# An 8-head half of a projection by Strassen's seven products, in a hybrid S5/RG-LRU decoder layer on Trainium2

## The chip, the core and the metric

The kernel runs on one core of a Trainium2 chip. The metric is the device time of one execution in microseconds (us), as the median of several runs. A profiled execution gives a trace of every engine: TensorE (PE: matmuls; PEld: its weight loads), VectorE (DVE), ScalarE (ACT), GpSimd (POOL) and SyncE (SP), which here only issues DMAs. DMAs are also issued from POOL.

## The reference: what is computed

One decoder layer on 1024 tokens of width 1024, everything in float32. Two branches run side by side and are merged by gates:

```
h = rms_norm(x, g_pre)
s5_x, s5_g, lru_x, lru_g, gate_s, gate_l = split(h @ w_in)
glu_a, glu_b = split(gelu(s5_ssm(s5_x)) @ w_glu)             # 512 -> 2 x 512
z_s = (glu_a * sigmoid(glu_b) * silu(s5_g)) @ w_bs           # 512 -> 1024
y_l = rg_lru(causal_conv(lru_x))                             # 10 heads of 128
z_l = (y_l * silu(lru_g)) @ w_bl                             # 1280 -> 1024
merged = sigmoid(gate_s) * z_s + sigmoid(gate_l) * z_l
x = x + rms_norm(merged @ w_out, g_post)                     # 1024 -> 1024
x = x + (p @ w_ple) * sigmoid(x @ w_ple_gate)
```

The change is in `z_l`, the product with w_bl: 10 input blocks (the heads) by 8 output blocks (rows d = 0 to 7) of 128 x 128.

## The kernel before

**Layout.** Activations are kept transposed, channels on the 128 partitions and the 1024 tokens (NT) along the free dimension, in two halves of 512 (HT). A product of a weight block with half the tokens is one matmul of 128x128 by 128x512.

**Three matmuls for one.** Both sides are kept as a high part (rounded to the matmul's type fp32r) and a low part, the remainder. `three` (L307 to 311) issues high x high, high x low and low x high, so a row of w_bl for both halves is 10 heads x 2 halves x 3 = 60 matmuls, and all of w_bl 480. `split` makes the parts of an operand: the high part by ACT's copy, the low part by DVE's subtraction (L305).

**Weights** (class `Weights`, L124 to 246). All blocks lie in one array in the order of use. SP loads chunks of up to 8 blocks (512 KB, L157) into four raw buffers. Four blocks make a quad: ACT copies the high part (L216) and DVE subtracts the low part (L228) into a ring of six quads; for w_bs, w_out and w_ple_gate the low part is made by an ACT copy of the negative (L219) and an adding DMA issued from POOL (L220). `W.ahead()`, called before a quad's matmuls, makes the quad four further on, its low part with the call after, and fetches and sums beyond that.

**Strassen's products in w_out.** For w_out the kernel already uses the Winograd form of Strassen's scheme. A 2 x 2 arrangement is made of the operand (two halves of the rows k, two halves of the tokens: B11, B12, B21, B22) and of the weights of two output rows (A11 to A22). Seven products replace eight; the weight sums S1 to S4 are made on POOL (`sum`, L173 to 205, the addition at L188), the operand differences T1 to T4 on DVE, and the products go to PSUM banks of their own which DVE adds into SBUF.

**Order of the work.** PE, ACT, DVE and POOL run in the order in which the program lists the instructions; SP's order is chosen by a scheduler, and it runs in that order too, so that a DMA that waits holds those behind it. Small pieces of work for DVE and ACT are written as generators in a list `bg`; `tick()`, called between products, lets each go on by one step, and `drain()` finishes them. The stages on PE are: w_ple, w_in's S5 columns, the gates (with the S5 recurrence beside), the ten LRU heads, then

- w_bl rows 0 and 1 together and row 2 (`bl`, L1097 to 1109), while `gel_build` splits the S5 outputs (L1083 to 1092);
- w_glu, four pairs eb and ea (L1128 to 1141): ACT takes the sigmoid of eb, DVE multiplies ea into `ysf` (L1138), and both split it into `ys`;
- w_bl rows 3 to 7, each followed by DVE's product with its gate (L1108) and a store to DRAM (`ms_d`); `yl_last` fetches head 9 again, whose place was lent;
- w_bs, eight rows F (L1231 to 1236): DVE multiplies the row by its gate `sgs_d`, loaded one to three rows ahead, into `mg` (L1234), and a DMA from POOL adds the w_bl row from `ms_d` onto it (L1235); `merged` (L1207) splits the sums and makes the differences for w_out;
- w_out: the X products (oX), then oY, oZ, oW, oV for each pair of rows; then w_ple_gate.

The operands of w_bl, `yl`, are made by head: heads 0 to 5 inside the LRU stage (L1039 to 1042), 6 to 9 after its end (L1068 to 1074). Before that loop DVE still has the product of the last gate column (`sg`, L952).

**PSUM.** `px` holds two banks, `pw2` three tiles of two banks (`wide`). After the last row F, `pw2` is closed and a pool `pp` of six single banks is opened in its place (L1237 and 1238; `bank`, L313), so that the first bank can be written once everything in `pw2` has been read.

Of the kernel before, what the change touches and what calls it, by code (L numbers as in the profile page):

```python
# [36 lines left out]
def weight_plan():  # L37
# [39 lines left out]
    plain(col("w_in", 7, range(ND)))  # L77
    for d in range(ND):
        if d == 3:
            for j in range(NS):  # L80
                plain(col("w_glu", 4 + j, range(NS)) + col("w_glu", j, range(NS)))
        if d == 0:
            for ks in (range(0, 4), range(4, 8), range(8, 10)):
                plain(col("w_bl", 0, ks) + col("w_bl", 1, ks))
        elif d > 1:
            for ks in (range(0, 8), range(8, 10)):
                plain(col("w_bl", d, ks))
    for n in range(0, ND, 2):
# [158 lines left out]
def tile_hybrid_trunk(  # L247
# [14 lines left out]
    px = ctx.enter_context(tc.tile_pool(name="px", bufs=2, space=PSUM))  # L262
    wide_ctx = ExitStack()
    pw2 = wide_ctx.enter_context(tc.tile_pool(name="pw2", bufs=3, space=PSUM))
    W = Weights(ctx, tc, w)
# [3 lines left out]
    def page(i, name, dt=F32R):  # L269
        return page_pool[i].tile([P, 2 * NT], dt, tag=f"pg{i}", name=name)  # L270
# [5 lines left out]
    ms_d = dram.tile([ND, P, NT], F32, name="ms_d")  # L276
    yl_d = dram.tile([P, NT], F32, name="yl_d")
    u_d = dram.tile([NS, 8, 16, 8, P], F32, name="u_d")
# [33 lines left out]

    def bank(name):  # L313
        return pp.tile([P, HT], F32, tag="pp", name=name)

    def wide(name):
        return pw2.tile([P, NT], F32, tag="pw2", name=name)

    bg = []
# [658 lines left out]
    l1 = lctx.enter_context(tc.tile_pool(name="l1", bufs=1))  # L978
    yl_home = {m: i for m, i in enumerate((2, 3, 6, 7, 8, 9, 4, 5, 10, 11))}
    yl, yl_raw = {}, {}  # L980

    def yl_page(m):
        t = page(yl_home[m], f"yl{m}", F32).rearrange("p (s n) -> p s n", s=2)
        yl[m] = t.bitcast(F32R)
        return t

    def lru_head(m):
# [33 lines left out]
        def late():  # L1021
            S.activation(ta, r, AF.Tanh, scale=sp8[:, m:m + 1])
            V.tensor_tensor(i, i, c, ALU.mult)
            S.activation(r, r, AF.Exp, scale=nsp8[:, m:m + 1])
            S.activation(sq, r, AF.Square)
            yield
            V.scalar_tensor_tensor(ta, sq, 1.0, ta, ALU.add, ALU.mult)
            S.activation(ta, ta, AF.Sqrt)
            yield
            V.tensor_tensor(i, i, ta, ALU.mult)  # L1030
            V.tensor_tensor_scan(sq, r, i, 0.0, ALU.mult, ALU.add)
            yield
            t = l1.tile([P, NT], F32, tag=f"yr{m}", name=f"yr{m}") if m in (6, 7) else g
            V.tensor_tensor(t, sq, g, ALU.mult)
            yl_raw[m] = t
            if m == NL - 1:
                nc.sync.dma_start(yl_d, t)
            if m < 6:
                yl_page(m)  # L1039
                S.activation(yl[m][:, 0], t, AF.Copy)  # L1040
                yield
                V.tensor_tensor(yl[m][:, 1], t, yl[m][:, 0].bitcast(F32), ALU.subtract)

# [12 lines left out]
    def gel_load():  # L1056
        for i in range(2):
            gel.append(page(i, f"gel{i}", F32).rearrange("p (b n) -> p b n", b=2))
        for b in range(NS):
            v = gel[b // 2][:, b % 2].rearrange("p (j k) -> p j k", j=8)  # L1060
            for g in range(8):
                nc.sync.dma_start(v[16 * g:16 * g + 16], y_d[b][:, :, g].rearrange("j c k -> c j k"))
# [4 lines left out]
    gel_load()  # L1067
    for m in range(6, NL):  # L1068
        t = yl_page(m)
        if m % 2:  # L1070
            V.tensor_copy(yl[m][:, 0], yl_raw[m])
        else:
            S.activation(yl[m][:, 0], yl_raw[m], AF.Copy)
        V.tensor_tensor(yl[m][:, 1], yl_raw[m], t[:, 0], ALU.subtract)
    lctx.close()
# [17 lines left out]

    def ylr(k, h):
        return yl[k][:, 0, HALF[h]], yl[k][:, 1, HALF[h]]

    def bl(ds):  # L1097
        gs = {}
        for d in ds:
            gs[d] = h2.tile([P, NT], F32, tag=f"g{d % 2}", name=f"blg{d}")  # L1100
            nc.sync.dma_start(gs[d], sgl_d[d])
        if len(ds) > 1:
            ps = [wide(f"ps_bl{d}") for d in ds]
            two(NL, ylr, "bl", ps=[[t[:, HALF[h]] for h in range(2)] for t in ps])
        else:
            ps = [rows(ylr, f"bl{ds[0]}", nk=NL)]
        for t, d in zip(ps, ds):
            V.tensor_tensor(gs[d], gs[d], t, ALU.mult)  # L1108
            nc.sync.dma_start(ms_d[d], gs[d])

    bg.append(gel_build())
    bl((0, 1))
    bl((2,))
    drain()

    ysf = [page(i, f"ysf{i}", F32).rearrange("p (k n) -> p k n", k=2) for i in range(2)]
# [6 lines left out]
    et = page(11, "et", F32).rearrange("p (i n) -> p i n", i=2)  # L1123

    def ger(k, h):
        return geo[k][:, 0, HALF[h]], geo[k][:, 1, HALF[h]]

    def by_slot(t):  # L1128
        return t.rearrange("p (k j) -> p j k", j=8)

    ys = []
    for j in range(NS):
        t, y = et[:, j % 2], ysr(j)
        pb = rows(ger, f"eb{j}", nk=NS)
        S.activation(by_slot(t), pb.rearrange("p (j k) -> p j k", j=8), AF.Sigmoid)
        V.tensor_tensor(t, t, y, ALU.mult)
        pa = rows(ger, f"ea{j}", nk=NS)
        V.tensor_tensor(by_slot(y), by_slot(t), pa.rearrange("p (j k) -> p j k", j=8), ALU.mult)  # L1138
        ys.append(page((16, 17, 18, 0)[j], f"ys{j}").rearrange("p (s n) -> p s n", s=2))
        S.activation(ys[j][:, 0], y, AF.Copy)  # L1140
        V.tensor_tensor(ys[j][:, 1], y, ys[j][:, 0].bitcast(F32), ALU.subtract)

    def yl_last():
        t = yl_page(NL - 1)
        nc.sync.dma_start(t[:, 1], yl_d)
        yield
        V.tensor_copy(yl[NL - 1][:, 0], t[:, 1])
        V.tensor_tensor(yl[NL - 1][:, 1], t[:, 1], t[:, 0], ALU.subtract)

    bg.append(yl_last())  # L1150
    for d in range(3, ND):
        bl((d,))
    drain()

    mpg = ((7, 8, 12, 13), (14, 15, 16, 17))

# [6 lines left out]
    def mgrow(d):  # L1163
        return mgt[d // 2][:, d % 2]
# [6 lines left out]
    def op(name, i):  # L1171
        mop[name] = [quarter(page(i + s, f"m{name}{s}")) for s in range(2)]

# [18 lines left out]

    mgt = [page(3 + i, f"mg{i}", F32).rearrange("p (k n) -> p k n", k=2) for i in range(4)]
    op("T2", 12)
    op("T3", 14)
    tmp = quarter(page(1, "mtmp", F32))
    gsp = page(11, "gsp", F32).rearrange("p (k n) -> p k n", k=2)
    late, gls = [], []

    def sgs_load():  # L1200
        n = len(gls)
        if n < ND:
            g = gsp[:, n // 2 % 2] if n % 2 else h2.tile([P, NT], F32, tag=f"g{n // 2 % 2}", name=f"gs{n}")
            nc.sync.dma_start(g, sgs_d[F_ROWS[n]])
            gls.append(g)

# [21 lines left out]

    for _ in range(3):
        sgs_load()  # L1230
    for n, d in enumerate(F_ROWS):  # L1231
        sgs_load()
        ps = rows(ysr_, f"F{d}", nk=NS)
        V.tensor_tensor(mgrow(d), gls[n], ps, ALU.mult)  # L1234
# [29 lines left out]
    def last_op():  # L1264
        op("T4", 12)
        for k in range(4):
            op_split("T4", k, mg(21, k))
            if k % 2:
                yield
        flush()  # L1270
        for i in (3, 4, 5, 6):
            x1p.append(page(i, f"x1{i}", F32).rearrange("p (k n) -> p k n", k=2))
        for k in range(ND):
            nc.sync.dma_start(x1p[k // 2][:, k % 2], x[k * P:(k + 1) * P, :])
# [6 lines left out]
    def mixt(row, h):  # L1281
        if mix[h][row // 4] is None:
            mix[h][row // 4] = quarter(page(((0, 2), (18, 11))[h][row // 4], f"mix{h}{row // 4}", F32))
        return mix[h][row // 4][:, row % 4, :]
# [121 lines left out]

    dg = quarter(page(1, "diags", F32))
    bg.append(post_half(1))
    for name, row in (("T4", 1), ("T4", 3), ("T4", 5), ("T4", 7), ("B21", 4), ("B21", 6)):
# [3 lines left out]
        squares[0].append(c)  # L1413
    plp, sbp = (quarter(page(i, n, F32)) for i, n in ((9, "plp"), (10, "sbp")))
    drain()
# [67 lines left out]
```

## Time and profile before

| | us |
|---|---|
| median of 3 runs | 962.28 |
| lowest, highest | 960.95, 965.21 |
| the profiled execution | 961.16 |
| its span in the trace | 959.4 |
| clock granted to TensorE | 0.999 |
| w_bl rows 0 to 2, on PE | 582.0 to 622.8 |
| w_glu | 622.8 to 667.0 |
| w_bl rows 3 to 7 | 667.0 to 735.0 |
| w_bs (F) | 735.0 to 779.2 |
| w_out | 780.8 to 861.5 |

The span runs from the first to the last recorded instruction; 1.76 us of the profiled execution lie outside it. Times of single instructions count from the span's start. A line of a timeline gives start, length, engine, source line, operation, and what it writes <- what it reads; "x4" are four instructions in a row, and a bracket at the end is the engine's idle time before it and what ended it. A matmul's recorded length is not its price, since matmuls overlap: the price is the distance between starts.

### The profile page before, as it was taken

To read this page: it belongs to the slowest core of one execution; us is meant where nothing else is said; L and a number is where in the kernel's file an instruction comes from. 1 tells how busy PE (TensorE), PEld (TensorE's weight loads), DVE (VectorE), ACT (ScalarE), POOL (GpSimd) and SP (SyncE) were. 2 spreads that over 40 slices of the span, in tenths; PEclk is the share of its full clock that TensorE was granted. 3 is DMA by queue.
4 is the path that set the end of the run, shared out by engine and by line. 5 is a ranking of instruction groups with operands and counts; after the bars stand their busy time and mean duration, and the time that the engine had idled before them with its cause. 6 is when DMAs were issued, how large, how long until landed. Compare 5 with 4: busy or idle time off the path is not lost.

```text
span 959.4 us, 11815 instructions
## 1 busy us (share of the span) xinstructions
PE 945.0 (98%) x4308; PEld 775.4 (81%) x4308; DVE 598.8 (62%) x1019; ACT 452.7 (47%) x652; POOL 161.0 (17%) x178
## 2 busy tenths in 40 slices
PE   8999999999999999999999999999999999999998
PEld 6888888788888888888888888888888877887877
DVE  6976578788763337766666668245311469786842
ACT  6652243344343256676666665224112344558561
POOL 1318121222210000000000000000001244534431
PEclk9999999999999999999999999999999999999999
DMA  9754133323333201111111115742347995399995
GB/s 347 256 129 125 51 117 116 116 73 116 117 116 99 71 28 50 50 50 45 50 50 50 50 50 150 262 153 63 109 148 219 236 224 174 116 244 231 283 256 156
DMA packets 64282, 128.19 MB, mean 134 GB/s; under 512 B 18400, under 2 KB 29024, under 8 KB 64224
## 3 DMA queue, kind: packets, MB, share of 16 engines
q1 hardware_dynamic: 55584, 109.61, 35.2%
q0 software_dynamic: 8640, 17.83, 10.5%
q8 instruction: 34, 0.56, 0.2%
q14 instruction: 24, 0.20, 0.1%
HBM read 84.81 MB, written 27.79 MB: 117 GB/s over the span
## 4 chain that ended last, share of the span: by engine, by line
PE 77%; DVE 10%; issue 7%; DMA 2%; ACT 2%; POOL 1%; SPq 1%; POOLq 0%; DVEq 0%; ACTq 0%
PE ps_L L309 6%; PE ps_L L311 5%; PE ps_L L310 5%; PE ps_rx L309 4%; PE ps_rg L309 4%; PE ps_rg L311 4%; PE ps_rx L311 4%; PE ps_rg L310 4%; PE ps_rx L310 4%; PE ps_bl L310 4%; PE ps_bl L309 4%; PE ps_bl L311 4%; PE ps_pg L310 2%; PE ps_pg L311 2%; PE ps_pg L309 2%
## 5 line engine op out<-in xcount | busy, mean ns | idle before, releaser
L216 ACT ACTIVATE wq<-wraw 128x512 fp32r<-128x512 f32 (+1 forms) x189 | 112.3, 606 | 90.3 <-PE ps_bl L311 77.6
L220 POOL DMA_DIRECT2D wq<-wraw x52 | 47.8, 920 | 533.3 <-ACT wq L219 516.9
L309 PE MATMUL ps_L<-hB,wq 128*128 128x512 f32 x320 | 127.1, 397 | 0.0
L311 PE MATMUL ps_L<-hB,wq 128*128 128x512 f32 x320 | 124.7, 390 | 0.0
L310 PE MATMUL ps_L<-hB,wq 128*128 128x512 f32 x320 | 124.7, 390 | 0.0
L228 DVE TENSOR_TENSOR wq<-wraw,wq 128x512 fp32r<-128x512 f32 (+1 forms) x137 | 97.1, 728 | 4.7 <-ACT wq L216 4.7
L309 PEld LDWEIGHTS ps_L<-hB,wq 128*128 128x128 f32 x320 | 60.1, 188 | 13.4 <-issue 1.7
L311 PEld LDWEIGHTS ps_L<-hB,wq 128*128 128x128 f32 x320 | 60.1, 188 | 12.9
L310 PEld LDWEIGHTS ps_L<-hB,wq 128*128 128x128 f32 x320 | 60.1, 188 | 11.7
L997 DVE SCALAR_TENSOR_TENSOR c<-ps_rx,cp_t,c 128x1023 f32<-128x1023 f32 (+2 forms) x30 | 38.4, 1282 | 43.6 <-ACT c L995 42.9
L309 PE MATMUL ps_rx<-hB,wq 128*128 128x512 f32 x160 | 62.5, 391 | 0.0
L309 PE MATMUL ps_rg<-hB,wq 128*128 128x512 f32 x160 | 62.5, 391 | 0.0
L311 PE MATMUL ps_rx<-hB,wq 128*128 128x512 f32 x160 | 62.4, 390 | 0.0
L311 PE MATMUL ps_rg<-hB,wq 128*128 128x512 f32 x160 | 62.4, 390 | 0.0
L309 PE MATMUL ps_bl<-yl,wq 128*128 128x512 f32 x160 | 62.3, 389 | 0.0
L311 PE MATMUL ps_bl<-yl,wq 128*128 128x512 f32 x160 | 62.3, 389 | 0.0
L310 PE MATMUL ps_rx<-hB,wq 128*128 128x512 f32 x160 | 62.2, 389 | 0.0
L310 PE MATMUL ps_rg<-hB,wq 128*128 128x512 f32 x160 | 62.2, 389 | 0.0
L310 PE MATMUL ps_bl<-yl,wq 128*128 128x512 f32 x160 | 62.2, 389 | 0.0
L1108 DVE TENSOR_TENSOR blg<-blg,ps_bl 128x1024 f32<-128x1024 f32 x8 | 9.8, 1221 | 68.8 <-PE ps_bl L311 68.7
L950 ACT ACTIVATE sg<-ps_L 128x1024 f32<-128x1024 f32 x20 | 20.5, 1026 | 61.6 <-PE ps_L L311 45.1
L310 PE MATMUL ps_pg<-x1hl,wq 128*128 128x512 f32 x120 | 47.4, 395 | 0.8 <-DVE x1hl L1185 0.8
(347 smaller groups left out, 2184.7 us busy)
## 6 DMA issues: line engine op xcount, KB each, us to landing
wraw<-w_blocks SPq DMA_DIRECT2D x90, 512.0 KB, 4.1
wq<-wraw POOLq DMA_DIRECT2D x52, 256.0 KB, 6.6
xt<-x_t SPq DMA_DIRECT2D x8, 512.0 KB, 8.2
ple_d<-ple_sb SPq DMA_DIRECT2D x8, 512.0 KB, 4.9
sgl_d<-sg SPq DMA_DIRECT2D x8, 512.0 KB, 4.8
sgs_d<-sg SPq DMA_DIRECT2D x8, 512.0 KB, 4.6
blg<-sgl_d SPq DMA_DIRECT2D x8, 512.0 KB, 4.7
ms_d<-blg SPq DMA_DIRECT2D x8, 512.0 KB, 3.0
```

The lines of the kernel that those rows point to most:

```text
L216: nc.scalar.activation(hi, src, AF.Copy)
L220: nc.gpsimd.dma_start(lo.bitcast(F32), src, accum_op=ALU.add)
L228: self.nc.vector.tensor_tensor(lo, src, hi.bitcast(F32), ALU.subtract)
L309: T.matmul(ps, wh, xh, start=start, stop=False, skip_group_check=more)
L310: T.matmul(ps, wh, xl, start=False, stop=False, skip_group_check=more)
L311: T.matmul(ps, wl, xh, start=False, stop=stop, skip_group_check=more)
L950: S.activation(t, ps, AF.Sigmoid)
L997: V.scalar_tensor_tensor(c[:, d:], ps[:, :NT - d], w_[3 - d], c[:, d:], ALU.mult, ALU.add)
L1108: V.tensor_tensor(gs[d], gs[d], t, ALU.mult)
```

## The change

Heads 0 to 7 of w_bl are computed by the same seven products as w_out, for four pairs of output rows; heads 8 and 9 ("tail") stay plain. For each pair p the products that use A11 with B11 (X, kept as U) and A12 with B21 are made right after the LRU stage, the token half 0 of the even rows, and their tails are added; then w_glu; then for each pair T2, T1, tail V, T3, tail W, B22, tail Z, T4. Unlike in w_out, sums are made in PSUM: DVE adds U to Z (L1256) and to W (L1261), and the next products accumulate onto the same banks. Parts:

- **Weights:** `weight_plan` lists the w_bl quads in the new order, 24 of them as sums ("O2", "S1", "S3", "S4") or parts of Strassen chunks; a pair makes four additions on POOL (L192 of the changed kernel).
- **Operands:** the LRU heads 0 to 7 keep their unsplit rows `yr`; B11 is split within the LRU stage, with the differences of the tokens' halves; B21 and heads 8 and 9 at its end; T2 and T1 during w_glu (`t_ops`); T3 ahead of the first pair, B22 and T4 in it, and the splits of `ys`, which had followed each ea, after them (`late_ops`).
- **PSUM:** `pw2` stays open for the whole kernel and `bank` hands out its halves; `pp` is gone.
- **Gates of w_bs:** the first four rows of `sgs_d` are loaded in the last pair, and each further one four rows ahead; F and w_glu are evicted by halves.
- Head 9's trip through DRAM (`yl_d`) is gone; pages are numbered anew (`PG`).

The diff, cut to its core:

```diff
+    for ks in (lo, hi):
+        for m in (0, 4):
+            plain(col("w_bl", m, ks) + col("w_bl", m + 2, ks))
+    plain([b for m in range(0, ND, 2) for b in col("w_bl", m, hi2)])
...
+    for m in range(0, ND, 2):
+        c0, c1 = (chunk(col("w_bl", m + i, range(8))) for i in range(2))
+        for part in ("O2", "S1", "P", "S3", "S4", "A22"):
+            if part == "P":
+                plain(col("w_bl", m, hi2) + col("w_bl", m + 1, hi2))
+            else:
+                quads.append((part, c0, c1, 4))
...
-    def bank(name):
-        return pp.tile([P, HT], F32, tag="pp", name=name)
+    def bank(name):
+        if spare:
+            return spare.pop()
+        t = wide(name)
+        spare.append(t[:, HT:])
+        return t[:, :HT]
...
-    for m in range(6, NL):
-        t = yl_page(m)
-        if m % 2:
-            V.tensor_copy(yl[m][:, 0], yl_raw[m])
-        else:
-            S.activation(yl[m][:, 0], yl_raw[m], AF.Copy)
-        V.tensor_tensor(yl[m][:, 1], yl_raw[m], t[:, 0], ALU.subtract)
+    bop("B21", 0, 1)
+    for k in range(4):
+        bsplit("B21", k, bq(21, k))
+    for m in (8, 9):
+        yl[m] = page(m - 4, f"yl{m}").rearrange("p (s n) -> p s n", s=2)
+        split(yl[m][:, 0], yl[m][:, 1], yl_raw[m])
...
+    for p_ in range(4):
+        bprod(xs[p_], "B11", True)
+        S.activation(bu[:, p_, :], xs[p_], AF.Copy)
+        tick()
...
+    for p_ in range(4):
+        bprod(xs[p_], "B21", False)
+        tick()
...
+        for h, ps in enumerate(brows(ger, f"ea{j}", NS)):
+            V.tensor_tensor(by_slot(y, h), by_slot(t, h), slots(ps), ALU.mult)
...
+    def late_ops():
+        for name, i, j, q in (("T3", 12, 13, 12), ("B22", 14, 15, 22), ("T4", 0, 1, 21)):
+            bop(name, i, j)
+            for k in range(4):
+                bsplit(name, k, bq(q, k))
+            yield
+        yield
+        for j in range(NS):
+            ys.append(page(PG[(16, 17, 18, 0)[j]], f"ys{j}").rearrange("p (s n) -> p s n", s=2))
+            for h in range(2):
+                split(ys[j][:, 0, HALF[h]], ys[j][:, 1, HALF[h]], ysr(j)[:, HALF[h]])
+                yield
...
+        z, w_, v = (bank(f"b{n}{p_}") for n in "ZWV")
+        bprod(z, "T2", True)
+        V.tensor_tensor(z, z, u, ALU.add)
+        S.activation(u, z, AF.Copy)
+        tick()
+        bprod(w_, "T1", True)
+        S.activation(gb[:, HT:], w_, AF.Copy)
+        V.tensor_tensor(w_, w_, u, ALU.add)
+        tick()
+        W.ahead()
+        wb = W.next()
+        btail(v, wb[2:], 1, True)
+        bmul(z, "T3", 2)
+        S.activation(u, z, AF.Copy)
+        V.tensor_tensor(v, v, gb[:, HT:], ALU.add)
+        V.tensor_tensor(v, v, u, ALU.add)
+        brow(m + 1, 1, ga[:, HALF[1]], v)
+        tick()
+        btail(w_, wb[:2], 1, False)
+        bmul(w_, "B22", 2)
+        brow(m, 1, gb[:, :HT], w_)
+        tick()
+        btail(z, wb[2:], 0, False)
+        bmul(z, "T4")
+        brow(m + 1, 0, ga[:, HALF[0]], z)
+        tick()
...
-        ps = rows(ysr_, f"F{d}", nk=NS)
-        V.tensor_tensor(mgrow(d), gls[n], ps, ALU.mult)
+        for h, ps in enumerate(brows(ysr_, f"F{d}", NS)):
+            V.tensor_tensor(mgrow(d)[:, HALF[h]], gls[n][:, HALF[h]], ps, ALU.mult)
         G.dma_start(mgrow(d), ms_d[d], accum_op=ALU.add)
         bg.append(merged(d))
-    wide_ctx.close()
-    pp = ctx.enter_context(tc.tile_pool(name="pp", bufs=6, space=PSUM))
```

`bprod` and `bmul` are a product of one quad with one operand, onto an empty bank or onto what it holds; `btail` is heads 8 and 9; `brow` multiplies a half row by its gate and stores it:

```diff
+    def bprod(ps, name, start):
+        W.ahead()
+        hi, lo = bops[name]
+        for k, wb in enumerate(W.next()):
+            three(ps, wb, (hi[:, k, :], lo[:, k, :]), start and k == 0, k == 3, not start)
...
+    def brow(d, h, gt, ps):
+        V.tensor_tensor(gt, gt, ps, ALU.mult)
+        nc.sync.dma_start(ms_d[d][:, HALF[h]], gt)
```

DVE's order at the end of the LRU stage, before, from the product of the last gate column on (`wq105` to `wq108` are the low parts of weight quads):

```order
L952 TENSOR_TENSOR sg_7_4569<-sg_7_4569,ps_L7_4499 128x1024
L1074 TENSOR_TENSOR yl6_4607<-yr6_4083,yl6_4607 128x1024
L1071 CAST yl7_4610<-yr7_4249 128x1024
L1074 TENSOR_TENSOR yl7_4610<-yr7_4249,yl7_4610 128x1024
L1074 TENSOR_TENSOR yl8_4613<-g8_4088,yl8_4613 128x1024
L1071 CAST yl9_4616<-g9_4254 128x1024
L1074 TENSOR_TENSOR yl9_4616<-g9_4254,yl9_4616 128x1024
L228 TENSOR_TENSOR wq105_4538<-wraw59_4301,wq105_4538 128x512
L228 TENSOR_TENSOR wq106_4632<-wraw60_4385,wq106_4632 128x512
```

The same place on DVE after the change (`bB211` is the low part of operand B21, `bB210` its high part; `yr` are the unsplit rows):

```order
L960 TENSOR_TENSOR sg_7_4569<-sg_7_4569,ps_L7_4499 128x1024
L307 TENSOR_TENSOR bB211_4608<-yr2_3750,bB210_4607 128x512 x2
L307 TENSOR_TENSOR bB211_4608<-yr3_4083,bB210_4607 128x512 x2
L307 TENSOR_TENSOR yl8_4617<-yr8_4414,yl8_4617 128x1024
L307 TENSOR_TENSOR yl9_4620<-yr9_4567,yl9_4620 128x1024
L232 TENSOR_TENSOR wq105_4538<-wraw59_4302,wq105_4538 128x512
L232 TENSOR_TENSOR wq106_4633<-wraw60_4386,wq106_4633 128x512
```

The four wide low parts and two casts give way to four half-wide lows of B21 and two wide lows; wq105, behind them in both, now belongs to the fourth X product.

DVE's order in the first w_bl row after w_glu (row 3), before (`yl9` is head 9 fetched again):

```order
L1147 CAST yl9_5146<-yl9_5146 128x1024
L1148 TENSOR_TENSOR yl9_5146<-yl9_5146 128x1024
L228 TENSOR_TENSOR wq122_5131<-wraw69_4878,wq122_5131 128x512
L228 TENSOR_TENSOR wq123_5162<-wraw70_5096,wq123_5162 128x256
L1108 TENSOR_TENSOR blg3_5128<-blg3_5128,ps_bl3_5130 128x1024
```

The same place after the change, from the eviction of the last w_glu row to the addition onto W of the first pair (`bZ0` names the PSUM tile that holds Z and W; `bu` is U; T3 and B22 are operands, their low parts written here):

```order
L1206 TENSOR_TENSOR ysf1_4826<-et_4831,ps_ea30_5083 128x4x128 x2
L307 TENSOR_TENSOR bT313_5118<-yr0_3076,bT312_5117 128x512 x2
L307 TENSOR_TENSOR bT313_5118<-yr1_3413,bT312_5117 128x512 x2
L232 TENSOR_TENSOR wq123_5084<-wraw68_4839,wq123_5084 128x512
L1256 TENSOR_TENSOR bZ0_5131<-bZ0_5131,bu_4630 128x512
L307 TENSOR_TENSOR bB2215_5151<-yr2_3750,bB2214_5150 128x512 x2
L307 TENSOR_TENSOR bB2215_5151<-yr3_4083,bB2214_5150 128x512 x2
L232 TENSOR_TENSOR wq124_5133<-wS2_120_4950,wq124_5133 128x512
L232 TENSOR_TENSOR wq125_5160<-wraw68_4839,wq125_5160 128x512
L1261 TENSOR_TENSOR bZ0_5131<-bZ0_5131,bu_4630 128x512
```

Between the additions onto Z and onto W stand the four lows of B22 and two weight lows; before, DVE touched PSUM only after a whole row.

More of the change, by code (lines that the diff above doesn't have):

```diff
@@ L1092, in gel_build @@
             yield
[L1094 to L1109, printed above, removed]
@@ L1111, in tile_hybrid_trunk, with btail @@
-    bg.append(gel_build())
-    bl((0, 1))
-    bl((2,))
-    drain()
-    ysf = [page(i, f"ysf{i}", F32).rearrange("p (k n) -> p k n", k=2) for i in range(2)]
+    def bprod(ps, name, start):
+        W.ahead()
+        hi, lo = bops[name]
+        for k, wb in enumerate(W.next()):
+            three(ps, wb, (hi[:, k, :], lo[:, k, :]), start and k == 0, k == 3, not start)
+    def btail(ps, wb, h, start):
+        for k, w_ in zip((8, 9), wb):
+            three(ps, w_, (yl[k][:, 0, HALF[h]], yl[k][:, 1, HALF[h]]), start and k == 8, k == 9, not start)
@@ L1118, in ysr @@
+    ysf = [page(10 + i, f"ysf{i}", F32).rearrange("p (k n) -> p k n", k=2) for i in range(2)]
     def ysr(j):
@@ L1122, in tile_hybrid_trunk, with brows @@
         nc.sync.dma_start(ysr(j), sil_d[j])
-    et = page(11, "et", F32).rearrange("p (i n) -> p i n", i=2)
+    et = page(0, "et", F32).rearrange("p (i n) -> p i n", i=2)
+    btmp = quarter(page(1, "btmp", F32))
+    bg.append(t_ops())
     def ger(k, h):
         return geo[k][:, 0, HALF[h]], geo[k][:, 1, HALF[h]]
-    def by_slot(t):
-        return t.rearrange("p (k j) -> p j k", j=8)
-    ys = []
+    def brows(rhs, name, nk):
+        ps = [bank(f"ps_{name}{h}") for h in range(2)]
+        for k in range(nk):
+            if k % 4 == 0:
+                W.ahead()
+                wb = W.next()
+            for h in range(2):
+                three(ps[h], wb[k % 4], rhs(k, h), k == 0, k == nk - 1)
+            if k % 2:
+                tick()
+        return ps
@@ new lines, in tile_hybrid_trunk, with sgs_load, bmul @@
+    PG = (9, 18, 11, 2, 3, 16, 17, 4, 5, 12, 13, 10, 14, 15, 0, 1, 6, 7, 8)
+    late_bl = late_ops()
+    next(late_bl)
+    bg.append(late_bl)
+    gls = []
+    gsp = []
+    def sgs_load():
+        n = len(gls)
+        if n < ND:
+            g = gsp[n // 2 % 2][:, n % 2]
+            nc.sync.dma_start(g, sgs_d[F_ROWS[n]])
+            gls.append(g)
+    def bmul(ps, name, held=1):
+        W.ahead(held)
+        hi, lo = bops[name]
+        for k, b in enumerate(W.next()):
+            three(ps, b, (hi[:, k, :], lo[:, k, :]), False, k == 3, True)
@@ new lines, in tile_hybrid_trunk @@
+    for p_ in range(4):
+        m, u = 2 * p_, bu[:, p_, :]
+        ga = h2.tile([P, NT], F32, tag="g0", name=f"ga{p_}")
+        gb = h2.tile([P, NT], F32, tag="g1", name=f"gb{p_}")
+        nc.sync.dma_start(ga, sgl_d[m + 1])
+        nc.sync.dma_start(gb[:, :HT], sgl_d[m][:, HALF[1]])
+        if p_ == 3:
+            gsp.extend(page(10 + i, f"gsp{i}", F32).rearrange("p (k n) -> p k n", k=2) for i in range(2))
+            for _ in range(4):
+                sgs_load()
+        z, w_, v = (bank(f"b{n}{p_}") for n in "ZWV")
[7 more added lines that the diff above has]
+        tick()
+        W.ahead()
+        wb = W.next()
+        btail(v, wb[2:], 1, True)
[8 more added lines that the diff above has]
+        brow(m, 1, gb[:, :HT], w_)
+        tick()
+        btail(z, wb[2:], 0, False)
+        bmul(z, "T4")
+        brow(m + 1, 0, ga[:, HALF[0]], z)
+        tick()
@@ L1171, in op @@
     def op(name, i):
-        mop[name] = [quarter(page(i + s, f"m{name}{s}")) for s in range(2)]
+        mop[name] = [quarter(page(PG[i + s], f"m{name}{s}")) for s in range(2)]
     def lagged(lo, src, hi, eng=None, copy=False):
@@ L1191, in tile_hybrid_trunk @@
     op("B21", 9)
-    mgt = [page(3 + i, f"mg{i}", F32).rearrange("p (k n) -> p k n", k=2) for i in range(4)]
+    mgt = [page(PG[3 + i], f"mg{i}", F32).rearrange("p (k n) -> p k n", k=2) for i in range(4)]
     op("T2", 12)
     op("T3", 14)
[L1196 to L1205, printed above, removed]
+    tmp = quarter(page(PG[1], "mtmp", F32))
+    late = []
     def merged(d):
@@ L1282, in mixt @@
         if mix[h][row // 4] is None:
[L1283 removed]
+            mix[h][row // 4] = quarter(page(PG[((0, 2), (18, 11))[h][row // 4]], f"mix{h}{row // 4}", F32))
         return mix[h][row // 4][:, row % 4, :]
```

112 lines of the change are left out of this document (64 added, 48 removed).

## The prediction

> **What bounds the kernel now.** I read the page's head first, then the windows by stage, the waits of PE, and the spacing of the matmuls of the stage that changes.
>
> ```profile
> span 959.4 us, 11815 instructions
> PE 945.0 (98%) x4308; PEld 775.4 (81%) x4308; DVE 598.8 (62%) x1019; ACT 452.7 (47%) x652; POOL 161.0 (17%) x178
> ```
>
> TensorE is busy for 98% of the span, so the time is the number of matmuls by their spacing, plus the few holes. The windows below are, in order, w_bl rows 0 to 2; w_glu; w_bl rows 3 to 7; w_bs (F); all of w_out; and a part of w_out's Strassen loop. Columns: stretch, length, busy time of PE, PEld, DVE, ACT, POOL, granted clock, DMA share, GB/s.
>
> ```profile
> 582.00:622.80 40.80, 40.80 (x182) 33.78 (x181) 22.22 (x24) 12.65 (x17) 0.00 (x0) 1.00 0.61 213
> 622.80:667.00 44.20, 44.20 (x194) 36.02 (x193) 21.13 (x19) 15.10 (x14) 0.00 (x0) 1.00 0.33 109
> 667.00:735.00 68.00, 68.00 (x301) 56.30 (x300) 16.45 (x20) 12.70 (x22) 4.47 (x5) 1.00 0.46 138
> 735.00:780.50 45.50, 44.37 (x193) 35.86 (x191) 21.87 (x27) 14.89 (x26) 12.29 (x14) 1.00 1.00 240
> 780.50:861.50 81.00, 79.03 (x352) 64.75 (x353) 69.40 (x102) 42.27 (x76) 35.58 (x30) 1.00 0.69 186
> 797.00:833.00 36.00, 35.76 (x157) 29.00 (x156) 32.65 (x43) 15.75 (x29) 18.45 (x13) 1.00 0.42 141
> ```
>
> In the three stretches that the change rewrites (582 to 735) PE never pauses, and the other engines have half their time or more free. So fewer matmuls there shorten the span one for one, unless a wait appears. The holes near the change are two, both where w_bs hands over to w_out:
>
> ```profile
> PE oX L310 <- DVE mB L1185: 1.5, 1, 1.5
> PE oX L309 <- DVE mg L1234: 1.4, 1, 1.4
> ```
>
> **Matmuls removed.** w_bl goes from 480 to 432 matmuls: heads 0 to 7 take 7 x 4 products of 12 (336) instead of 384, heads 8 and 9 keep 96. The price of one is the spacing of starts in rows 3 to 7, where PE streams without a pause (first and last start, per line of the triple):
>
> ```profile
> L309 PE MATMUL ps_bl<-yl,wq x100: 389/389/398, 667.0 to 734.4; 128*128 128x512 f32 x100
> L311 PE MATMUL ps_bl<-yl,wq x100: 389/389/397, 667.5 to 734.8; 128*128 128x512 f32 x100
> L309 PE MATMUL ps_F<-ys,wq x64: 394/394/398, 735.0 to 778.5; 128*128 128x512 f32 x64
> L311 PE MATMUL ps_F<-ys,wq x64: 392/392/397, 735.5 to 779.0; 128*128 128x512 f32 x64
> ```
>
> From 667.0 to 734.8 lie 299 steps, 0.2267 us each: 48 x 0.2267 = **-10.9 us**. F's spacing is (779.0 - 735.0)/191 = 0.230, and w_out's loop, whose operands are differences as the new ones are, has 36/157 = 0.229. Should all 432 run like F, that is 432 x 0.0033 = +1.4; I take **+0.5**, for the third of them whose operands are split late beside much other traffic (range 0 to 1.4).
>
> **Operands at the end of the LRU.** Before, VectorE (DVE) goes through these (start, length):
>
> ```profile
> 585.62 1.21 DVE L952 TENSOR_TENSOR sg<-sg,ps_L 128x1024 f32<-128x1024 f32 x1
> 588.60 1.23 DVE L1074 TENSOR_TENSOR yl<-yr,yl 128x1024 fp32r<-128x1024 f32 x1
> 589.75 1.22 DVE L1074 TENSOR_TENSOR yl<-g,yl 128x1024 fp32r<-128x1024 f32 x1
> 592.75 2.49 DVE L228 TENSOR_TENSOR wq<-wraw,wq 128x512 fp32r<-128x512 f32 x4
> ...
> 762.80 0.68 DVE L1185 TENSOR_TENSOR mB<-mg,mB 128x512 fp32r<-128x512 f32 x1
> 763.40 0.69 DVE L1221 TENSOR_TENSOR mg<-mg,mg 128x512 f32<-128x512 f32 x1
> ```
>
> A wide operation takes 1.15 from start to start, a half-wide one 0.60. After the sg product (free at 586.75) now come four B21 lows (2.4), the lows of yl8 and yl9 (2.3), and only then the low part of wq105 (0.6), the weights of the fourth product: about 592.1. The product starts after 36 matmuls, 582.0 + 36 x 0.2267 = 590.2, and its third matmul, the first to read the low part, at 590.6. That is **+1.5**; from 0, if the four B21 lows find their place before the sg product's wait ends, to 2.7, if their ACT halves are two wide operations late. Before, the queue was longer (it came to its four weight lows at 592.75) and no matmul waited, because a quad of weights then served 24 matmuls, both halves of the tokens, and now serves 12: wq105 was needed after 72 of them, at 598.3.
>
> **w_glu earlier.** It now begins after 120 matmuls instead of 180: 582.0 + 27.2 + 1.5 = 610.7, not 622.8. SyncE's queue sets what it needs:
>
> ```profile
> 587.25 13.87 SPq L1062 DMA_DIRECT2D gel<-y_d  x26
> 602.16 1.57 SPq L157 DMA_DIRECT2D wraw<-w_blocks  x3
> wraw<-w_blocks SPq DMA_DIRECT2D x10, 512.0 KB, 4.6
> ```
>
> The gel loads hold it until 601.1; the first w_glu load behind them lands 4.6 later, 605.7, and its two parts are done 1.2 after. So 3.8 of cover remain where there were 12: **0** (0 to 1.5, the last gel block's split standing behind those weights). DVE in w_glu takes 16 operand operations more, 9.7 us on 21.1 of 44.2: hidden.
>
> **The Strassen loop.** Let E be the end of the last w_glu product. In a pair T2 runs from E, T1 from 2.7, the V tail from 5.4, T3 from 6.8, the W tail from 9.5, B22 from 10.9. T3 accumulates into Z after DVE added U to it, the W tail after DVE added U to W.
>
> ```profile
> L1138 DVE TENSOR_TENSOR ysf<-et,ps_ea x4: 2266/2266/2266, 634.0 to 667.2; 128x1024 f32<-128x1024 f32 x4
> 785.07 0.61 ACT L1178 ACTIVATE mT<-mg 128x512 fp32r<-128x512 f32 x1
> 785.59 0.58 ACT L1312 ACTIVATE mix<-oX 128x512 f32<-128x512 f32 x1
> ```
>
> DVE first evicts the last w_glu row, by halves now; the first half is free before E, so it ends near E + 1.8. Four T3 lows: 4.2; wq123: 4.8; Z add: 5.4, in time for 6.8. Four B22 lows follow, but ACT writes their high parts after the copy of U that waits for the Z add: four times 0.58, to 8.1, then wq125's high part and the copy of W: 9.3. DVE's last B22 low ends at 8.9, wq124 and wq125 at 10.1, the W add at 10.8. PE wants W at 9.5 and gets it 1.3 late; with one sum on POOL in the way, 2.3 or more (below). I take **+1.8** in the first pair. In the later pairs the T3, B22 and T4 splits are done, two ys lows stand in their place, and W is ready some 2 us early: **0**; the bounds are 0 and four times 1.8.
>
> Each pair also has four weight sums on POOL. What they do to DVE shows where w_out's loop begins, and inside it:
>
> ```profile
> 788.07 1.63 POOL L188 TENSOR_TENSOR wS<-wraw 128x512 f32<-128x512 f32 x1
> ...
> 814.54 1.80 POOL L188 TENSOR_TENSOR wS<-wraw 128x512 f32<-128x512 f32 x1 [2.43 <-DVE wq L228]
> ```
> ```profile
> 787.95 2.30 DVE L1223 TENSOR_TENSOR mg<-mg,mtmp 128x512 f32<-128x512 f32 x1
> 790.18 3.48 DVE L1185 TENSOR_TENSOR mT<-mg,mT 128x512 fp32r<-128x512 f32 x2
> ...
> 815.09 0.68 DVE L1338 TENSOR_TENSOR mix<-mix,oV 128x512 f32<-128x512 f32 x1
> 815.69 0.68 DVE L1325 TENSOR_TENSOR mix<-mix,oY 128x512 f32<-128x512 f32 x1
> ```
>
> An operation with both inputs in SBUF beside a sum takes 2.30 instead of 0.68, the sum's 1.63 more; two take 3.48 instead of 1.3. An add that reads PSUM keeps its 0.68. The loop's DVE work is 24 weight lows, 20 splits and 28 operations on PSUM, 72 x 0.60 = 43; with 16 sums that hold it 1.63 each (26), 69 of 70.7. [...]
>
> **From w_bs to w_out.** The merged PSUM pool takes away the wait of the first oX matmul for the last gate product. The next wait remains:
>
> ```profile
> 779.40 1.22 DVE L1234 TENSOR_TENSOR mg<-gsp,ps_F 128x1024 f32<-128x1024 f32 x1 [0.72 <-PE ps_F L311]
> 783.81 0.69 DVE L1218 TENSOR_TENSOR mtmp<-mg,mg 128x512 f32<-128x512 f32 x1 [2.58 <-DMA mg<-ms_d]
> 794.90 0.68 DVE L1185 TENSOR_TENSOR mB<-mg,mB 128x512 fp32r<-128x512 f32 x1
> ```
>
> The last gate product, its accumulating DMA and DVE's queue lead to the B21 low at 795.58, for which oX waits; this chain hangs on F's end and not on the pool, so the idle time moves from the first hole to the second. Taking the product by halves ends it 0.6 sooner, and the DMA engines, busy at 1.00 in the F stretch, have four of the eight gate loads behind them: **-0.7** (0 to -2). The 16 half stores of ms_d and the loads of ga and gb wait for each other on SyncE (2.7 and 4.9 to landing), more than 5 us ahead of what PE needs.
>
> ```profile
> blg<-sgl_d SPq DMA_DIRECT2D x5, 512.0 KB, 4.9
> ms_d<-blg SPq DMA_DIRECT2D x3, 512.0 KB, 2.7
> ```
>
> **Sum.** -10.9 + 0.5 + 1.5 + 0 + 1.8 - 0.7 = -7.8. The profiled execution took 961.16, its span 959.4 with 1.76 around it; so 953.4 there. The median, 962.28, stands 1.1 above that: **954.5**. With every stall hidden it is 962.28 - 10.9 - 2.0 = 949.4.
>
> **Rivals.** What a measurement of this kernel can tell from no change is about 0.5%, 4.8 us: faster is below 957.5, slower above 967.1.
>
> *The wait for W in every pair.* If the two ys lows and the two weight lows ahead of the W add keep it late in the later pairs as in the first, 3 x 1.8 = 5.4 come on top: 959.9, no change that can be told. For it: DVE's work is in the program's order, and the W add stands behind lows that nobody needs yet. Against it: their high parts are written a product earlier there. 0.19.
>
> *All stalls hidden.* wq105 in time, W in time: 949.4 to 951. For it: in w_out's loop, with DVE busy 32.65 of 36, PE stood for only 0.24. 0.15.
>
> *Slower: the sums hold DVE on PE's path.* All four sums of a pair stop a low ahead of the Z or W add: 4 x 1.63 = 6.5 a pair, 26 in all: 962.28 - 10.9 + 2.0 + 26 - 0.7 = 978.7. It decides from 14.3 us in all on (4.8 and the 9.5 that is left of the gain without the pair term), 3.6 a pair, more than two of four sums. For it: unlike w_out's, these products accumulate onto what DVE has added, so PE itself waits. Against it: the 0.24 above, beside 13 operations on POOL. 0.07.
>
> *No saving:* that PE keeps 480 matmuls' time through slower spacing (0.252) has no row for it; 0.02, near 962.
>
> The forecast has 0.57, its own range 951 to 957.4. Faster is 0.57 + 0.15 = 0.72, no change 0.19 + 0.02 = 0.21, slower 0.07. The range is 949 to 961.5: it takes in the full gain and the first rival; the slow one stays out.
>
> **What would show it.** Right: no pause of more than 0.3 within the four pairs after the first, W's first tail matmul waiting 1 to 2 us for the add once, the fourth X product about 1.5 for wq105, oX's first wait gone and the second longer by most of it, spacing 0.227 to 0.230. Wrong: PE waits for an add or a weight low in each pair; sums on POOL beside stretched lows just ahead of them; w_glu's first matmul waiting for geo or its weights; or DVE waiting for ga.

## The result, and the profile after

The changed kernel takes 1026.96 us (median of 4 runs, 1024.69 to 1027.38), the kernel before 961.62: a ratio of 1.0668, 95% interval 1.0635 to 1.0702. It is slower by 65 us where 8 less were forecast, and outside the range.

The head of the profile after, and its windows by stage. The columns are those of the windows before: stretch, length, busy time of PE, PEld, DVE, ACT, POOL, granted clock, DMA share, GB/s. The stretches are the X products, w_glu, the four pairs, F, w_out, and w_ple_gate.

```profile
span 1022.9 us, 11949 instructions
PE 953.9 (93%) x4260; PEld 773.4 (76%) x4260; DVE 634.9 (62%) x1102; ACT 477.4 (47%) x709; POOL 184.2 (18%) x194
```

```profile
581.10:621.90 40.80, 30.18 (x121) 23.56 (x120) 20.30 (x25) 18.20 (x27) 0.00 (x0) 0.92 0.48 159
621.90:666.20 44.30, 44.30 (x194) 36.08 (x193) 31.68 (x37) 19.28 (x28) 7.41 (x5) 1.00 0.34 118
666.20:758.40 92.20, 76.35 (x314) 58.73 (x313) 46.71 (x70) 31.59 (x57) 20.02 (x16) 0.98 0.47 150
758.40:801.90 43.50, 43.50 (x193) 36.04 (x192) 20.46 (x33) 14.57 (x26) 10.58 (x13) 1.00 0.93 212
801.90:915.90 114.00, 89.64 (x354) 69.50 (x353) 68.75 (x104) 43.34 (x78) 39.22 (x34) 0.91 0.54 143
915.90:1022.90 107.00, 94.10 (x425) 75.59 (x423) 53.10 (x79) 52.02 (x94) 32.33 (x34) 0.98 0.81 202
```

The first thing to see is where the time was lost. The X products take 40.8 us for 120 matmuls (27.2 at 0.2267), the pairs 92.2 for 312 (70.7). But w_out, of which the change touches nothing but the PSUM banks, goes from 80.7 to 114.0 us, and w_ple_gate, at the very end, from 97.9 to 107.0. Two thirds of the loss lie outside w_bl. The other engines are about as busy in w_out as before (DVE 68.75 us against 69.40): PE simply stands there for 24 us, and its clock is down to 0.91. The waits of PE (total, times, longest):

```profile
PE ps_pg L311 <- ACT sbp L1506: 8.8, 7, 2.4
PE bX L311 <- ACT bu L1135: 8.1, 2, 7.4
PE oV L311 <- DVE mix L1528: 6.0, 3, 3.0
PE bZ L311 <- ACT bu L1257: 5.3, 2, 3.9
...
PE oX L311 <- ACT mix L1428: 4.6, 1, 4.6
PE oW L311 <- ACT sq L1409: 4.4, 3, 1.5
PE bW L311 <- DVE ga L1126: 4.3, 2, 2.1
```

All are at line 311, the first matmul of `three`, where a product or its tail begins, and they wait for instructions that read the product before: ACT's copy of X0 into U (`bu`), DVE's gate product, ACT's sigmoid of a w_ple_gate row. (The oW line names ACT's square of a row in SBUF; DVE's last addition from oW, which does read PSUM, ends within 0.1 us of it.) The first one, on PE's timeline:

```profile
591.39 0.80 PE L311 MATMUL bX<-bB,wq 128*128 128x512 f32 x1 [7.39 <-ACT bu L1135]
591.99 0.63 PE L312 MATMUL bX<-bB,wq 128*128 128x512 f32 x1
592.41 0.63 PE L313 MATMUL bX<-bB,wq 128*128 128x512 f32 x1
592.84 0.63 PE L311 MATMUL bX<-bB,wq 128*128 128x512 f32 x1
...
598.10 0.39 PE L311 MATMUL bX<-bB,wq 128*128 128x512 f32 x1
598.33 0.39 PE L312 MATMUL bX<-bB,wq 128*128 128x512 f32 x1
```

And on ACT's:

```profile
590.75 0.60 ACT L1135 ACTIVATE bu<-bX 128x512 f32<-128x512 f32 x1 [3.40 <-DVE yl L307]
```

X1 begins as soon as X0 has been copied, though it goes to another bank. The copy itself stands back until DVE is done with yl9 (`bu` lies where the LRU stage's buffers were). After the wait the matmuls start 0.427 us apart for 8 of them, then 0.227 again.

**Theory A:** the new `bank` hands out the two halves of one two-bank tile, and the program's waits are kept by tile: the first matmul into one half waits for the reader of the other half, so each odd product waits for the drain of the product before. **Theory B,** the rival: the Strassen loop costs the time itself, through POOL's sums and the additions on PSUM for which PE waits, and w_out suffers from work that runs on into it.

### The profile page after: what moved, and what is told of

It is laid out like the page before. It is cut to its first block, busy times and chain, and to the rows that moved or that the text cites. A ratio compares the mean times of both kernels' runs of the same rounds, so it can differ in the third digit from the quotient of the medians.

```text
span 1022.9 us, 11949 instructions
## 1 busy us (share of the span) xinstructions
PE 953.9 (93%) x4260; PEld 773.4 (76%) x4260; DVE 634.9 (62%) x1102; ACT 477.4 (47%) x709; POOL 184.2 (18%) x194
## 4 chain that ended last, share of the span: by engine, by line
PE 69%; DVE 13%; issue 8%; ACT 5%; DMA 2%; POOL 2%; SPq 1%; ACTq 0%; POOLq 0%; DVEq 0%
PE ps_L L311 4%; PE ps_L L313 4%; PE ps_L L312 4%; PE ps_rg L311 4%; PE ps_rx L311 4%; PE ps_rg L313 4%; PE ps_rx L313 4%; PE ps_rx L312 4%; PE ps_rg L312 4%; PE ps_pg L311 2%; PE ps_pg L313 2%; PE ps_pg L312 2%; PE ps_u L312 1%; PE ps_u L313 1%; DVE q L912 1%
## 5 line engine op out<-in xcount | busy, mean ns | idle before, releaser
L232 DVE TENSOR_TENSOR wq<-wraw,wq 128x512 fp32r<-128x512 f32 (+1 forms) x136 | 93.7, 703 | 16.2 <-ACT wq L220 16.1
L192 POOL TENSOR_TENSOR wS<-wraw 128x512 f32<-128x512 f32 x8 | 12.1, 1519 | 395.9 <-DMA wraw<-w_blocks 368.6
L1019 DVE SCALAR_TENSOR_TENSOR c<-ps_rx,cp_t,c 128x1023 f32<-128x1023 f32 (+2 forms) x30 | 38.5, 1282 | 48.8 <-ACT c L1017 48.1
L311 PE MATMUL ps_pg<-x1hl,wq 128*128 128x512 f32 (+1 forms) x128 | 50.7, 396 | 8.8 <-ACT sbp L1506 8.8
L313 PE MATMUL ps_pg<-x1hl,wq 128*128 128x512 f32 (+1 forms) x128 | 50.1, 391 | 0.0
L312 PE MATMUL ps_pg<-x1hl,wq 128*128 128x512 f32 (+1 forms) x128 | 50.0, 391 | 0.0
L1507 DVE TENSOR_TENSOR sbp<-sbp,plp 128x512 f32<-128x512 f32 (+1 forms) x17 | 12.5, 738 | 41.8 <-ACT sbp L1506 41.8
```

The costliest lines, as they stand in the source:

```text
L192: G.tensor_tensor(s[name], s[a], s[b], op)
L232: self.nc.vector.tensor_tensor(lo, src, hi.bitcast(F32), ALU.subtract)
L311: T.matmul(ps, wh, xh, start=start, stop=False, skip_group_check=more)
L312: T.matmul(ps, wh, xl, start=False, stop=False, skip_group_check=more)
L313: T.matmul(ps, wl, xh, start=False, stop=stop, skip_group_check=more)
L1019: V.scalar_tensor_tensor(c[:, d:], ps[:, :NT - d], w_[3 - d], c[:, d:], ALU.mult, ALU.add)
```

## The experiments

**Single banks from w_bl on.** Everything of the change stays, but the banks are tiles of their own:

```diff
     def bank(name):
+        if pps:
+            return pps[0].tile([P, HT], F32, tag="pp", name=name)
         if spare:
...
+    wide_ctx.close()
+    pps.append(ctx.enter_context(tc.tile_pool(name="pp", bufs=6, space=PSUM)))
     xs = [bank(f"bX{p}") for p in range(4)]
```

> The changed kernel, with one edit: at the end of the LRU stage the pool of two-bank tiles is closed and a pool of six single-bank tiles is opened, as the kernel before did ahead of w_out; everything else of the change stays. Theory A (both halves of a two-bank tile are one object for the waits, so the first matmul into one half waits for the reader of the other): the waits of Z, W, oX to oV and ps_pg for ACT and DVE go; w_out takes 81 us again and w_ple_gate 98, the w_bl loop 71 to 74; the first X product now waits about 5 us for the last gate column to be read; 955 to 962 in all. Theory B (the sums of the Strassen loop itself cost the time: POOL's sums and the adds on PSUM that PE waits for): the stretch from the LRU's end to F stays near 177 us, w_out and w_ple_gate alone gain; about 985.

It took 963.7 us (before: 962.87; ratio 1.0007, 0.9994 to 1.0019): 63 us of the loss are gone with one edit. The waits that remain:

```profile
PE bX L312 <- DVE sg L963: 4.7, 1, 4.7
PE oX L313 <- DVE mB L1317: 2.5, 1, 2.5
PE oX L312 <- ACT mB L1310: 1.7, 1, 1.7
...
PE bW L312 <- DVE bW L1266: 1.2, 1, 1.2
```

The first is the price of opening the pool there, as expected; 13 matmuls at the wider spacing follow it (about 2.5 us), which were not. None of the waits for the reader of another product is left. It came out 1.7 us above theory A's range and far from theory B's 985.

**Single banks from w_out on.** The same edit, but with the two lines that open the pool after the last row F.

> The changed kernel, with the six single-bank tiles opened only after the last row F, so that halves of two-bank tiles are still handed out in w_bl, w_glu and F. Theory A: w_out back from 114 to 81 us and w_ple_gate from 107 to 98, the w_bl stretch as slow as in the changed kernel, the hole ahead of oX back with up to 3 us: 985 to 990. Theory B says the same of w_out only if the lost time there came from the tiles as well; if it came from w_bl's late work running on into w_out, w_out stays near 114 and the whole near 1027.

988.26 us (1.0261, 1.0245 to 1.0278), 39 less than the changed kernel. From oX to the first w_ple_gate product it takes 81.6 us (805.7 to 887.3) and 98.3 from there to the end, as before; from the first X product to F 177.6 (583.0 to 760.6), against 177.3 in the changed kernel: the loss follows the tiles, stage by stage.

**The kernel before with shared tiles.** No Strassen in w_bl; only the pool `pp` is dropped and `bank` hands out halves of `pw2`.

```diff
-    wide_ctx.close()
-    pp = ctx.enter_context(tc.tile_pool(name="pp", bufs=6, space=PSUM))
```

> The kernel before, with nothing of Strassen in w_bl; only the two-bank tiles stay open to the end and their halves serve as the banks of w_out and w_ple_gate. Theory A: w_out 33 us and w_ple_gate 9 us longer, the wait of oX for the pool gone: 1000 to 1005. Theory B: no waits beyond the old ones, 960 to 962.

1001.06 us (1.0392, 1.0377 to 1.0407). With w_bl untouched, the same waits of w_out and w_ple_gate appear with nearly the same lengths; the windows are w_out and w_ple_gate:

```profile
PE ps_pg L308 <- ACT sbp L1394: 8.7, 7, 2.3
PE oV L308 <- DVE mix L1416: 6.0, 3, 3.1
PE oW L308 <- ACT sq L1297: 4.4, 3, 1.5
PE oX L308 <- ACT mix L1316: 4.0, 1, 4.0
```

```profile
778.70:892.50 113.80, 89.67 (x355) 69.42 (x354) 68.36 (x102) 43.09 (x77) 38.56 (x34) 0.93 0.54 141
892.50:999.20 106.70, 93.36 (x425) 75.66 (x423) 53.08 (x79) 51.96 (x94) 32.22 (x34) 0.98 0.82 203
```

That rules out theory B for these stages. Theory A stands from both sides: sharing alone slows the kernel before, and taking the sharing away heals the changed one.

**No shared tiles.** To have the Strassen part without the new wait of X0: X0, X1, Z0 and W0 go to the two single banks of `px`, which is idle then, X2 and X3 to one half each of a two-bank tile, and the single banks are opened for the first V.

```diff
-    xs = [bank(f"bX{p}") for p in range(4)]
+    xs = [inner(f"bX{p}") if p < 2 else wide(f"bX{p}")[:, :HT] for p in range(4)]
...
+        if p_ == 0:
+            z, w_ = inner("bZ0"), inner("bW0")
+            wide_ctx.close()
```

> The changed kernel without any two banks of one tile in use at different times: X0, X1, Z0 and W0 in the two single banks of the first PSUM pool, X2 and X3 in a two-bank tile each, of which one half stays empty, and the six single banks opened when the first pair's V needs one. Theory A: as the single-bank variant but without the wait of the first X product, so about 5 us faster than it: 950 to 957, the saving of 10.9 us less two or three small stalls. Theory B: 980 or more.

960.43 us (0.9967, 0.9954 to 0.9979): 2.4 less than the kernel before, but 3 us above theory A's range. Here the terms of the forecast can be read one by one. Its waits:

```profile
PE oX L313 <- DVE mB L1324: 2.5, 1, 2.5
PE bW L312 <- DVE bW L1273: 1.8, 1, 1.8
PE bX L314 <- DVE wq L232: 1.4, 1, 1.4
...
PE oX L312 <- ACT mB L1317: 1.1, 1, 1.1
```

The second and third are the forecast's two stalls, in place and size. What it did not have is the clock: matmuls 0.427 us apart behind the wait for W and behind that for mB.

**The two waits moved.** On that kernel, the weights' low parts ahead of the last splits, and the first pair's B22 splits behind the W add:

```diff
         bsplit("B21", k, bq(21, k))
+    W.ahead()
     for m in (8, 9):
...
         S.activation(u, z, AF.Copy)
-        tick()
+        if p_:
+            tick()
```

> The variant without shared tiles (960.4 us), with two moves on DVE and ACT: the weight low parts up to wq105 ahead of the splits of yl8 and yl9, and in the first pair the B22 splits behind the add onto W. If the prediction's two small stalls were right in place and cause, the waits of 1.4 us at the fourth X product and of 1.8 us at W's tail go, and with the second the 9 matmuls at 0.43 us spacing behind it (about 1.8 us): 5 us less, 955 to 956. If the W add was late because POOL's sums held DVE, it stays late by about as much, and only 1.5 us go: 959.

954.67 us (0.9914, 0.9901 to 0.9928), 0.3 below the expected range: the cause of the two stalls was rightly named. In the traces the X products go from 28.9 to 27.3 us and the pairs from 75.2 to 71.5, together 5.2 less. The four pairs now run without a pause, with all 16 sums on POOL:

```profile
653.50:725.00 71.50, 71.50 (x314) 58.45 (x313) 48.44 (x70) 31.35 (x57) 20.40 (x16) 1.00 0.61 181
```

**Row 7's B21 part first,** on that kernel and on the kernel before: the last row's split that oX waits for is made one tick earlier.

```diff
         yield
+        if d == 7:
+            op_split("B21", 3, mg(21, 3))
+            flush()
         yield
...
-        op_split("B21", k, mg(21, k))
+        if d < 7:
+            op_split("B21", k, mg(21, k))
```

> As the kernel with the two waits moved, and besides the last row's B21 part (row 7) is split one tick earlier, ahead of row 7's first difference and of row 6's T2. The two waits of oX (1.1 and 2.5 us) and the 13 matmuls at 0.43 us behind them (2.6 us) should go or fall below 1.5 us in all: 4 to 6 us less than the kernel with the two waits moved, 950 to 952. If the accumulating DMA of row 7 lands only then, DVE waits for it instead and less than 2 us are gained.

> The kernel before, with only the earlier split of row 7's B21 part. Its first oX wait (1.4 us, for the PSUM pool) stays, the second (1.5 us) goes or shrinks: 960.5 to 962. Its waits were too short to be followed by slow matmuls, so nothing more than the wait itself can be gained.

The first took 953.89 us (0.9908, 0.9896 to 0.9921), no more than 0.8 less: a miss. PE's wait at oX for DVE shrank from 2.5 to 0.8 us, but right behind it the low part of a w_out quad was late:

```profile
PE oX L313 <- DVE mB L1326: 0.8, 1, 0.8
PE oX L314 <- DMA wq<-wraw: 0.7, 1, 0.7
```

Its adding DMA, issued from POOL at 778.51, landed at 786.58. And the two short waits, 1.9 us apart, were still followed by 8 slow matmuls. The trace shows more than the median does: from the first oX to the first w_ple_gate product it takes 82.1 us, where the kernel with the two waits moved took 85.3. But this execution reached the X products 2.1 us later (583.4 against 581.3), ahead of everything that the edit touches; why isn't known, so the 0.8 can't be taken for what the edit is worth in w_out. The second kernel showed no change, 962.89 (0.9998, 0.9989 to 1.0007), 0.9 above the expected range: its oX wait for the PSUM pool stays and the other falls from 1.5 to 0.3, but two waits behind it, of 0.5 for an operand and 0.6 for a weight low, take its place.

**The sums doubled.** To price the forecast's slow rival, each w_bl sum runs twice on POOL in the kernel with the two waits moved:

```diff
+                if BLOCKS[q[1][0]][0] == "w_bl":
+                    d = self.tmp.tile([P, HT // 2], F32, tag="dup", name=f"wdup{name}_{i}")
+                    for h in (slice(0, HT // 2), slice(HT // 2, HT)):
+                        G.tensor_tensor(d, s[a][:, h], s[b][:, h], op)
                 G.tensor_tensor(s[name], s[a], s[b], op)
```

> The kernel with the two waits moved (954.7 us), and each of the 16 weight sums of w_bl preceded on POOL by the same sum once more, in two halves into a tile that nobody reads. If sums hold DVE for their whole length on PE's path (the prediction's slow rival), 16 more of 1.6 us or longer give up to 26 us: 965 to 980, with PE waiting for the Z or W adds in every pair. If the path has room for them, as the pairs without waits say, 954 to 956, and only DVE's own times beside the sums grow. In between, a wait for the sums' own chain (POOL to ACT to DVE to PE) of 1 to 4 us a pair would show as PE waiting for a weight low of T2.

958.13 us (0.9959, 0.9948 to 0.9971), between the two: about 3.5 us more; in the traces the four pairs take 74.4 us instead of 71.5. A window within the pairs and three groups of DVE's operations in it (busy, mean ns); the last line is the first group in the kernel with the two waits moved, over 654 to 725 us:

```profile
655.00:726.00 71.00, 69.41 (x299) 55.31 (x298) 54.86 (x70) 30.42 (x57) 40.05 (x35) 1.00 0.50 163
```

```profile
L236 DVE TENSOR_TENSOR wq<-wS,wq 128x512 fp32r<-128x512 f32 x10 | 11.1, 1115 | 0.0
L312 DVE TENSOR_TENSOR bB<-yr,bB 128x512 fp32r<-128x512 f32 x4 | 4.7, 1228 | 0.0
L1279 DVE TENSOR_TENSOR bW<-bW,bu 128x512 f32<-128x512 f32 x4 | 2.8, 689 | 2.2 <-ACT gb L1278 2.2
```

```profile
L232 DVE TENSOR_TENSOR wq<-wS,wq 128x512 fp32r<-128x512 f32 x10 | 7.6, 761 | 0.0
```

POOL's work in the pairs doubles from 20.4 to 40.05 us, and DVE's grows by 6.8 (48.1 to 54.9 over equal stretches of 71 us). Of the operations with two inputs in SBUF, the weight lows and the B22 lows stretch (the weight lows of the sums from 761 to 1115 ns, the B22 lows from 805 to 1228), those of `bT` (679 and 677) and `ys` (868 and 778) do not. The additions onto PSUM keep their 690. PE pauses for 1.6 of 71. DVE's busy time grew by about a third of POOL's added time (6.8 of 19.65 us), where the slow rival had counted all of it.

## Why the prediction was wrong, point by point

The step that failed is the sentence under "From w_bs to w_out": "The merged PSUM pool takes away the wait of the first oX matmul for the last gate product." It costed the merge by the wait that it removes, at -0.7 us, and not by what it ties together. The unit for which the program waits became twice as large everywhere that `bank` is used: in w_bl, in w_out and in w_ple_gate. The sign stood in the order ahead of the forecast, where Z and W carry one tile's name; a search through the first matmul of each product for what it now waits for would have found it.

How the loss adds up, from PE's timelines from 570 us on: a wait is the distance between two starts less 0.2267 where the profile marks an idle time or the distance is over 0.55, a slow matmul one that is followed after 0.30 to 0.55 us.

| | waits, us | slow matmuls, us |
|---|---|---|
| before | 5.4 | 2.0 |
| after | 66.1 | 16.2 |
| before, shared tiles | 36.5 | 10.4 |
| after, no shared tiles | 11.3 | 6.0 |
| the same, two waits moved | 9.0 | 4.1 |

After against before that is 60.7 + 14.2 = 74.9; less the 10.9 of the removed matmuls, 64.0, against the 63.5 by which the span grew.

The other terms, read where nothing is shared (958.8 us of span):

- *Matmuls removed, -10.9:* right. In the kernel with the two waits moved, X, w_glu and the pairs take 27.3, 44.9 and 71.5 us (581.3 to 725.0), 143.7 against 153.0 before: -9.3. Of the 1.6 that lack, 0.8 is wider spacing in the pairs (71.5 against 70.7), for which +0.5 stood in the sum, and 0.7 lies in w_glu, with the geo wait two points below.
- *The fourth X product, +1.5:* 1.4, for wq105 as said.
- *w_glu, 0:* no wait in the kernel without shared tiles, 0.4 for a geo part once X had become faster.
- *The W add, +1.8 once, 0 later:* 1.8 in the first pair, none in the others; the place is right, the size in part luck. With E = 655.5 the Z add ended at 661.6 (E + 6.1; forecast 5.4) and the W add at 667.1 (E + 11.6; forecast 10.8). DVE evicted both halves of the last w_glu row only after E, until E + 2.5 instead of 1.8, which added 0.7; and no sum on POOL stretched a low ahead of the W add, for which 0.5 had been allowed. What was missing were 9 slow matmuls behind the wait, 1.7 us.
- *From w_bs to w_out, -0.7:* the idle time did move from the first hole to the second, but it grew, from 2.9 to 3.6 us, and the longer wait was followed by 13 slow matmuls, 2.6 us, which the two shorter ones before were not. That is +3.3 instead of -0.7. The forecast had the chain's start wrong, too: DVE stood for the data of row 6, not of row 7, the last one (before, DVE went on at 783.81, and row 7's data landed at 787.93). Those of row 6 landed 5.4 us after F's end instead of 4.5, and all of DVE's queue came later by that; the halves of the last product could gain nothing there.
- *The rivals:* none of them was what happened. The slow one had the direction, but named POOL's sums. Beside all 16 of them the pairs of the kernel with the two waits moved run without a pause, 0.8 us over the 70.7 of the matmuls alone, and 16 more cost about 3.5: far from the 14.3 at which they would have decided.

So the forecast of 954.5 would have missed by 6 us without the shared tiles, 4.3 of it slow matmuls, and by 72 with them. That the kernel with two waits moved also stands at 954.7 is no support for the sum: its stalls differ.

What stays open: whether the chip itself would bear the matmul into one half beside the read of the other wasn't tried, since the wait alone cannot be taken away; only the tiles were changed. With single banks, of the same size as such a half, one product is written while another is read: in the kernel with the two waits moved PE is busy for all of the 71.50 us of the pairs, beside DVE's additions onto products that PE has left (those onto Z at 691 ns each).

## What to carry to other kernels

When buffers are merged into larger ones, ask of every user which other user's reader it now waits for: a wait that the merge removes at one place is small against a unit of waiting that doubles at all places, also in stages that the change doesn't name. Read the names of the tiles in the new order of instructions: where two products that follow each other have one name, the second waits for the drain of the first. And cost a stall of TensorE with what follows it: two waits of 1.4 and 1.5 us, 15 us apart, cost only themselves here, but waits of 1.1 and 2.5 with one matmul between them another 2.6 of slow matmuls.

## What the runs showed of the hardware

A wait of TensorE can be followed by slow matmuls. After the wait of 1.8 us for W in the kernel without shared tiles:

```profile
667.16 0.50 PE L312 MATMUL bW<-yl,wq 128*128 128x512 f32 x1 [1.82 <-DVE bW L1273]
667.50 0.45 PE L313 MATMUL bW<-yl,wq 128*128 128x512 f32 x1
667.74 0.63 PE L314 MATMUL bW<-yl,wq 128*128 128x512 f32 x1
668.17 0.63 PE L312 MATMUL bW<-yl,wq 128*128 128x512 f32 x1
...
670.73 0.58 PE L312 MATMUL bW<-bB,wq 128*128 128x512 f32 x1
671.14 0.39 PE L313 MATMUL bW<-bB,wq 128*128 128x512 f32 x1
```

The starts are 0.427 us apart from 667.74 to 670.73, then 0.227 again. The granted clock goes with them: it is 0.50 in this stretch and 1.00 ahead of it and behind it (columns as in the windows above).

```profile
664.00:667.10 3.10, 1.34 (x6) 0.75 (x4) 3.10 (x7) 3.10 (x7) 0.97 (x1) 1.00 0.00 0
667.75:671.10 3.35, 3.35 (x9) 2.63 (x8) 3.35 (x5) 2.59 (x5) 1.57 (x1) 0.50 0.38 139
671.50:676.00 4.50, 4.50 (x22) 3.68 (x21) 4.36 (x7) 1.79 (x3) 1.31 (x1) 1.00 0.16 58
```

In the trace of the changed kernel, from 570 us on, the six waits of 2.43 us or more (up to 7.39) were each followed by 7 to 11 matmuls with 0.40 to 0.45 us between starts; the wait of 2.09 us that ends at 904.85 was followed by 8, those of 2.03, 2.14 and 2.15 by none, and none of those from 0.69 to 1.76 was. In the kernel without shared tiles a wait of 1.82 was followed by slow ones, as the rows above show, and with row 7's part first so were the two of 0.8 and 0.7 close together.

The granted clock in the changed kernel's trace goes with these: from 570 us to the last 5 us it is 0.50 from 588.38 to 595.21, 673.72 to 677.13, 806.84 to 813.67, 820.49 to 823.90, 892.17 to 899.00, 905.83 to 909.24 and 963.85 to 967.26, and 1.00 for the rest. Behind the wait of 2.14 us that ends at 705.98 it is 1.00 (706.0 to 710.0), behind that of 2.09 that ends at 904.85 it is 0.50 (905.9 to 909.2). So of the waits of about 2 us the length alone does not tell which are followed by slow matmuls; what does was not shown.
